# A two-layer DiT on one core: the image tokens' FFN norms spread over the context's FFN, the context's last down products moved to that FFN's end, and one modulation moved from VectorE to ScalarE

## The chip, the core and the metric

One core of one Trainium2 chip runs the whole program. Its engines work side by side and meet by semaphores: PE (TensorE: matmuls, with its weight loads as PEld), DVE (VectorE), ACT (ScalarE), POOL (GpSimd), and SP (SyncE, which issues most of the DMAs). Each engine takes its instructions in the order in which they stand in its queue. The metric is the device time of one execution in microseconds (us); lower is better. The times are medians over runs.

## The reference

Two layers work on 512 image tokens `x` and 256 context tokens `ctx`, both 1024 wide, in float32. Cut to what matters here (the mixers before it are attention, a Fourier mix and a long convolution):

```python
def conv_ffn(h, w_up, w_c, b_c, w_down):
    u = dwconv3(h @ w_up, w_c, b_c)              # 1024 -> 2 x 2816, then a 3-tap conv along the tokens
    gate, val = jnp.split(u, 2, axis=-1)
    return (jax.nn.silu(gate) * val) @ w_down    # 2816 -> 1024

for i in range(2):
    ...
    x = x + ga1 * rmsnorm(mix_x, g_post_mix[i])
    if not last:
        ctx = ctx + cga1 * rmsnorm(mix_c, g_post_mix[i])
    fx = rmsnorm(x, g_pre_ffn[i]) * (1.0 + sc2) + sh2
    x = x + ga2 * rmsnorm(conv_ffn(fx, ...), g_post_ffn[i])
    if not last:
        fc = rmsnorm(ctx, g_pre_ffn[i]) * (1.0 + csc2) + csh2
        ctx = ctx + cga2 * rmsnorm(conv_ffn(fc, ...), g_post_ffn[i])
```

In layer 0 both streams pass the FFN; the context that comes out of it is normed and modulated again at the start of layer 1 (`rmsnorm(ctx, g_pre_mix) * (1 + csc1) + csh1`). In layer 1 only x does.

## The kernel before

**Matmuls.** Each float32 operand is split into a high and a low part (L179 casts the high part on ACT, L180 subtracts it on DVE or POOL), and each product is three matmuls: high by high, high by low, low by high (`mm3`, L194 to L196). Weights come from DRAM in tiles of 512 KB (names `r`, `Wr`, `L` while raw) and become `Wh` and `Wl`. Products gather in PSUM, in four tiles `pn` and two wide tiles `pw`.

**Order of the work.** The program is written as generators. `go(name, gen, bg)` runs one of them and gives the share `bg` of PE's time to background steps ("fillers") that were put into lanes with `add`; `need(name)` runs a filler to its end before what follows. Out of the sequence so written, the framework's scheduler fixes each engine's queue when the program is built, by its own simulation. After that nothing is reordered.

**The context's FFN** (`ffn_c`, layer 0 only) takes the 22 channel blocks m of 128 in 11 groups of two. `up(m)` makes gate and value (48 matmuls with 256 columns), the convolution (L655 on ACT, L656 and L657 on DVE), SiLU, the product with the value (L1301 on POOL) and the split into `gc`. Behind the first `up` of each group come the down products of the group before (24 matmuls with 512 columns), added into `y` (L1249 on DVE). The last group's down products are not run there: `ffn_c` only makes their generator and keeps it as `rest_c`.

**What rest_c does** (`ffn_down` with `end` true): it loads two down weights (their low halves split on POOL), runs 24 matmuls, adds to `y` (L1243, DVE), takes sums of squares (L231, ACT), multiplies by the gate `G` (L1245, POOL), and then hands each of the context's two token tiles to `tail`, which adds a filler `tail_c0` or `tail_c1`. Such a filler makes the root of the mean square (L221 to L227; the square root L222 on ACT needs its own function table, loaded by ACT_TABLE_LOAD), the residual (L1155, DVE), the same for the norm that follows, a diagonal `dg` of the norm's factors (L348, DVE), and `norm_tile`: PE turns the tile by matmuls with `dg` (`turn`, L361), the modulation (scale and shift for each channel) runs on DVE (L404) or ACT (L406), and the result is split into `h`. `norm_tile(..., dve)` gives the first `dve` of each four blocks to DVE.

**The norms of x** (`norm_tile7`, fillers `norm_xf0` to `norm_xf3`, one for each 128 tokens) turn by L361, modulate on DVE (L435), and form the sums and differences that the seven-product scheme below needs (L446, L447, L449, L451, with splits by `put`, some on POOL). They are added in the mixers' output stage. What has not been run as a filler by the end of `ffn_c` is run by `need("norm_xf3")` ahead of the FFN of x.

**The FFN of x** (`ffn_x`) uses a seven-product scheme (Strassen and Winograd's): for each m, `prep(m)` makes from the up weights four differences on POOL (L1348 to L1351, `tt`), whose high and low halves are made on ACT and DVE; `first(m)` runs two of the products, `rest(m)` the other five, with sums on ACT and DVE (L1391 to L1398, tile `C`). In layer 0 the first steps are `prep(0)`, `first(0)`, `prep(1)`, `first(1)`, then `rest(0)` and `rest(1)`. `RC` in the table `Z` says where `rest_c` runs: with 3, behind `rest(3)`.

The places that the prediction speaks of are thus: `ffn_c`, the seam between it and `ffn_x`, the place of `rest_c`, and the two fillers `tail_c0` and `tail_c1`, which take their turns among the products of `ffn_x`.

Of the kernel before, what the change touches and what calls it, by code (L numbers as in the profile page):

```python
# [46 lines left out]
def tok(ap):  # L47
    return ap.rearrange("p (a t) -> p a t", t=256)
# [6 lines left out]


RT = True
Z = {'HV': [[[0], [1]], [[0, 1], []], [[], [0], [], [1]]], 'go_mod00': 1.0, 'go_norm_c': 0.3, 'go_hyp_c': 0.5, 'go_kvf_c': 0.5, 'go_q_c': 0.5, 'go_out_c': 1.0, 'go_ffn_c': 0.1, 'go_ffn': [0.1, 0.1], 'SH0': [0.7, 0.7, 0.7, 0.4, 0.5], 'SH1': [0.7, 0.7, 0.7, 0.5, 0.5], 'w_norm_x': 0.0, 'w_attn_c': 0.0, 'w_four_c': 2.0, 'w_norm_cf': 12.0, 'w_gate00': 0.0, 'w_mod_f0': 0.0, 'w_mod10': 8.0, 'w_gate10': 0.0, 'w_mod_f1': 0.0, 'w_taps': 0.0, 'mlat1': 1.0, 'mlat0': 1.2, 'mlat2': 2.0, 'lat': 7.0, 'nt': 0.8, 'nt7': 0.8, 'mg': 2.0, 'hy0': 1.0, 'hy1': 7.0, 'hy2': 14.0, 'tp0': 9.0, 'tp1': 2.5, 'tp2': 1.5, 'tp3': 2.0, 'at0': 1.5, 'at1': 2.0, 'as': 3.5, 'lead': 1, 'wx1': 9.0, 'QK0': [3.0, 7.0, 3.0, 6.0], 'QK1': [5.0, 7.0, 3.0, 6.0], 'TC': [50.0, 10.0, 10.0], 'BG': [0.15, 0.3], 'WN': [9.0, 7.0], 'ND': [3, 4], 'GF': ['Wm', 2.0, 0.0], 'MD': [4, 4, 4, 4], 'DG': [15, 15, 0], 'RC': 3, 'TW': 0.5, 'KE': 4, 'MT': 3, 'PO': [['k', 'f', 'v'], ['f', 'k', 'v']], 'EF': 1, 'E0': 4, 'lane_k': 4, 'el_na': 2, 'el_nx1': 4, 'ec': 3, 'CT': ['T', 'Q', 'T'], 'FX': 1, 'OC': 'qhHkayf'}
NF = 2, 4
OR = "", "hcyqkf"  # L60
NC = None, 4
CE = True
CR = "LL"

# [1 line left out]
class Net:  # L66
# [218 lines left out]
    def mod_block(self, l, b, out, ahead=None, tag="Wm"):  # L285
# [11 lines left out]
        out.append(s)  # L297
        yield 0.44, Z["mg"]

# [81 lines left out]
    def norm_tile(self, st, t, n, AB, el=None, dve=4):  # L381
# [14 lines left out]
        for b in range(2):  # L396
# [10 lines left out]
            for i in range(4 // kp):  # L407
                j = 4 * b // kp + i
                self.hi = self.split(hi[j][:, a, :, ts], lo[j][:, a, :, ts], tf[:, i * kp * P : (i + 1) * kp * P].rearrange("p (k t) -> p k t", t=P), el).ins
            yield 4 * CTR, Z["nt"]  # L410

    def norm_tile7(self, st, t, n, AB):
# [6 lines left out]
        def put(name, src, el):  # L419
            if name not in st.S:  # L420
                st.S[name] = tuple(self.M("h").rearrange("p (k t) -> p k t", t=256) for _ in range(2))
            hi, lo = st.S[name]
            ts = slice(t % 2 * P, t % 2 * P + P)
            self.hi = self.split(hi[:, :, ts], lo[:, :, ts], src.rearrange("p (k t) -> p k t", t=P), el).ins
# [3 lines left out]
        for b in range(2):  # L428
            ps = self.pn()
            self.turn(ps, n, b)  # L430
            for k in range(4):
                c = slice(k * P, (k + 1) * P)
                a_, b_ = A[:, 4 * b + k, st.idx : st.idx + 1], B[:, 4 * b + k, st.idx : st.idx + 1]
                if k < Z["MD"][t]:
                    self.mod = nc.vector.tensor_scalar(dst[b][:, c], ps[:, c], a_, b_, op0=ALU.mult, op1=ALU.add).ins  # L435
                else:
                    nc.scalar.activation(dst[b][:, c], ps[:, c], AF.Identity, scale=a_, bias=b_)
            if t < 2:
                put(("11", "12")[b], dst[b], (nc.gpsimd, nc.vector)[t])
            yield 4 * CTR, Z["nt7"]  # L440
        if t < 2:
# [26 lines left out]
    def norm_all(self, st, xt, AB, pre=False):  # L468
# [8 lines left out]
        for t in range(st.NT):  # L477
            yield from self.norm_tile(st, t, xt[t], AB, self.nc.vector if pre else None, Z["el_na"])

# [89 lines left out]
    def post_q(self, st, qraw, qss):  # L569
# [3 lines left out]
        st.Q = [self.M("Q").rearrange("p (h t) -> p h t", t=st.T) for _ in range(NH // hp)]  # L573
        yield 0.0, Z["QK%d" % self.lay][0] + st.NT
        pend = []
# [888 lines left out]
    def run(self):  # L1464
# [27 lines left out]
        for l in range(2):  # L1492
# [107 lines left out]
            def tail_c(t, xr, ss):  # L1600
# [176 lines left out]
```

## Time and profile before

| what | us |
|---|---|
| time, median of 3 runs | 1768.56 (1767.65 to 1769.28) |
| profiled execution | 1770.96 |
| its span | 1769.2 |
| PE busy in it | 1640.4 |
| stretch 478 to 686.8 | the context's FFN |
| stretch 686.8 to about 1065 | the FFN of x, layer 0 |

The mean granted clock of the span was 0.969. The profile names instructions by line, engine and operation, then tiles (output, arrow, inputs) and shape. In a timeline the first number is the start and the second the length; a bracket holds the idle time before it and what ended it. In a group of instructions, behind the bar stand the busy time, the mean of one in ns, then the engine's idle time just before them and its releasers. In the waits of an engine, the numbers are the total, the count and the longest.

### The profile page before, as it was taken

What the parts mean: (1) busy time and instruction counts of PE and PEld (TensorE: products, weight loads), DVE (VectorE), ACT (ScalarE), POOL (GpSimd) and SP (SyncE); (2) the same over time, 40 slices, a digit from 0 to 9 for tenths busy, and PEclk for the clock granted to TensorE, in tenths of its full rate; (3) what the DMA queues carried; (4) which work ended last, traced back from release to release, by engine and by line L of the source; (5) the groups of instructions that cost most, each with busy time, mean ns of one, the idle gap of its engine ahead of it and who ended that gap; (6) DMA issues with size and microseconds to landing.
All of it is one profiled execution on the core that took longest, in us unless ns stands there. A gap on an engine that the chain in (4) does not pass through costs nothing. (4 is left out here: it accounts for less than half of the span.)

```text
span 1769.2 us, 27894 instructions
## 1 busy us (share of the span) xinstructions
PE 1640.4 (93%) x10534; PEld 1400.9 (79%) x10534; DVE 1391.0 (79%) x2269; ACT 949.8 (54%) x1787; POOL 672.2 (38%) x495
## 2 busy tenths in 40 slices
PE   6899988899999998998899998998899799999997
PEld 2677765787788897887889985787787678999995
DVE  3776667697666698888899997668895978989996
ACT  3554354586565454555555555534874455555553
POOL 2342212000134348664465545312002456555543
PEclk9899998999999998999999998999999799999999
DMA  9224377603476642233243358654012343323323
GB/s 361 92 77 140 88 226 267 231 11 143 164 254 229 227 153 82 86 108 96 72 138 113 96 168 320 214 176 132 1 48 82 128 137 119 105 88 106 96 74 129
DMA packets 75314, 246.69 MB, mean 139 GB/s; under 512 B 8111, under 2 KB 9647, under 8 KB 75180
## 3 DMA queue, kind: packets, MB, share of 16 engines
q1 hardware_dynamic: 66348, 215.54, 36.4%
q0 software_dynamic: 8832, 29.37, 5.4%
q8 instruction: 83, 1.36, 0.3%
q14 instruction: 51, 0.42, 0.1%
HBM read 230.72 MB, written 14.16 MB: 138 GB/s over the span
## 5 line engine op out<-in xcount | busy, mean ns | idle before, releaser
L194 PE MATMUL pn<-h,Wh 128*128 128x256 f32 x1328 | 374.4, 284 | 10.9 <-DVE C L1398 3.4
L196 PE MATMUL pn<-h,Wl 128*128 128x256 f32 x1328 | 370.2, 282 | 7.6 <-DVE Wl L180 7.6
L195 PE MATMUL pn<-h,Wh 128*128 128x256 f32 x1328 | 371.9, 281 | 1.9 <-POOL h L180 1.9
L194 PEld LDWEIGHTS pn<-h,Wh 128*128 128x128 f32 x1328 | 251.8, 190 | 21.2 <-issue 4.4
L196 PEld LDWEIGHTS pn<-h,Wl 128*128 128x128 f32 x1328 | 251.3, 190 | 11.7 <-DVE Wl L180 9.0
L195 PEld LDWEIGHTS pn<-h,Wh 128*128 128x128 f32 x1328 | 252.7, 190 | 5.9 <-POOL h L180 2.1
L179 ACT CAST Wh<-Wr 128x1024 fp32r<-128x1024 f32 x118 | 123.5, 1050 | 137.3 <-PE pn L195 63.1
L1348 POOL TENSOR_TENSOR tt<-r,r 128x512 f32<-128x512 f32 x44 | 66.0, 1501 | 260.7 <-DMA r<-w_up 224.8
L180 DVE TENSOR_TENSOR Wl<-Wr,Wh 128x1024 fp32r<-128x1024 f32 x89 | 121.5, 1367 | 53.2 <-ACT Wh L179 52.7
L195 PE MATMUL pw<-Wl,gT 128*128 128x512 f32 x352 | 141.0, 401 | 2.0 <-DVE Wl L180 2.0
L194 PE MATMUL pw<-Wh,gT 128*128 128x512 f32 x352 | 136.3, 403 | 5.3 <-ACT Wh L179 2.6
L196 PE MATMUL pw<-Wh,gT 128*128 128x512 f32 x352 | 139.7, 398 | 0.0
L180 DVE TENSOR_TENSOR Wl<-tt,Wh 128x1024 fp32r<-128x1024 f32 x88 | 129.8, 1495 | 7.5 <-ACT Wh L179 7.5
L1407 POOL TENSOR_TENSOR ft<-ft,ft 128x512 f32<-128x512 f32 x44 | 66.6, 1513 | 145.0 <-DVE ft L657 78.6
L179 ACT CAST Wh<-tt 128x1024 fp32r<-128x1024 f32 x88 | 91.1, 1047 | 51.5 <-PE pw L196 32.3
L180 POOL TENSOR_TENSOR h<-tf,h 128x256 fp32r<-128x256 f32 (+1 forms) x40 | 40.3, 1028 | 177.0 <-ACT h L179 177.0
L180 POOL TENSOR_TENSOR Wl<-Wr,Wh 128x1024 fp32r<-128x1024 f32 x29 | 72.8, 2516 | 61.3 <-ACT Wh L179 61.1
L1350 POOL TENSOR_TENSOR tt<-r,tt 128x512 f32<-128x512 f32 x44 | 83.9, 1907 | 13.5 <-DVE Wl L180 13.5
L655 ACT ACTIVATE ft<-C,vec 128x512 f32<-128x512 f32 x88 | 68.9, 811 | 34.3 <-DVE C L1395 20.0
L194 PE MATMUL pw<-h,Wh 128*128 128x256 f32 (+1 forms) x224 | 76.0, 339 | 9.8 <-DVE y L1249 2.7
L292 PE MATMUL pn<-wm,cpad 128*32 128x256 f32 x768 | 69.9, 433 | 15.2 <-DMA wm<-w_mod 14.9
L1278 DVE TENSOR_TENSOR y<-y,pw 128x1024 f32<-128x1024 f32 x64 | 77.3, 1212 | 7.8 <-PE pw L196 7.7
(379 smaller groups left out, 4696.6 us busy)
## 6 DMA issues: line engine op xcount, KB each, us to landing
wm<-w_mod SPq DMA_DIRECT2D x96, 512.0 KB, 5.0
r<-w_up SPq DMA_DIRECT2D x90, 512.0 KB, 3.6
Wr<-w_down SPq DMA_DIRECT2D x66, 512.0 KB, 3.9
L<-w_up SPq DMA_DIRECT2D x44, 512.0 KB, 4.3
Wr<-w_out SPq DMA_DIRECT2D x24, 512.0 KB, 3.6
Wr<-w_in_t SPq DMA_DIRECT2D x16, 512.0 KB, 3.9
dft<-hdft_x POOLq DMA_DIRECT2D x16, 512.0 KB, 4.1
Wr<-w_in_c SPq DMA_DIRECT2D x12, 512.0 KB, 3.6
```

The lines of the kernel that those rows point to most:

```text
L179: r = nc.scalar.copy(hi, src)
L180: (el or nc.vector).tensor_tensor(lo, src, f32(hi), op=ALU.subtract)
L194: nc.tensor.matmul(ps, l[0], r[0], start=first, stop=False, **kw)
L195: nc.tensor.matmul(ps, l[0], r[1], start=False, stop=False, **kw)
L196: nc.tensor.matmul(ps, l[1], r[0], start=False, stop=last, **kw)
L292: nc.tensor.matmul(ps[32 * g : 32 * g + 32, cs], self.cpad[:, q % 2 * 4 + g, :], w[:, g, :], start=q % 2 == 0, stop=q % 2 == 1, skip_group ...
L655: nc.scalar.activation(dst, ps, AF.Identity, scale=w1, bias=b)
L1278: nc.vector.tensor_tensor(y, y, ps, op=ALU.add)
L1348: te.tensor_tensor(half(t13, 0), half(r[1], 0), half(r[0], 0), op=ALU.subtract)
L1350: te.tensor_tensor(half(t24, 0), half(r[1], 1), half(t13, 0), op=ALU.subtract)
L1407: nc.gpsimd.tensor_tensor(o[0], o[0], o[1], op=ALU.mult)
```

## The change

Three things change, all in layer 0. First, `ffn_c` calls `need("norm_xf0")` ahead of its group 1, `norm_xf1` ahead of group 3, `norm_xf2` ahead of group 5 and `norm_xf3` ahead of group 7. Second, `rest_c` is a step of its own between `ffn_c` and `ffn_x`. Third, `norm_tile` in `tail_c` gets `dve` = 0, so all four blocks of each half are modulated by ACT (L406); that is 16 instructions which move from DVE to ACT. No other instruction is added or dropped but ACT_TABLE_LOADs, of which the program has 19 now and 21 before.

```diff
-Z = {'HV': ..., 'RC': 3, ...}
+Z = {'XS': [1, 3, 5, 7], 'HV': ..., 'RC': -2, ...}
...
-NC = None, 4
+NC = None, 0
...
         groups = [list(range(a, a + G)) for a in range(0, MF, G)]
         for i, ms in enumerate(groups):
+            if i in Z["XS"]:
+                self.need(f"norm_xf{Z['XS'].index(i)}")
             for j, m in enumerate(ms):
                 yield from up(m)
...
                 self.go("ffn_c", self.ffn_c(l), Z["go_ffn_c"])
+                if Z["RC"] == -2:
+                    self.go("rest_c", self.rest_c, Z["go_ffn_c"])
                 self.need("norm_xf3")
             self.go("ffn", self.ffn_x(l), Z["go_ffn"][l])
```

In the changed kernel the lines behind the first insertion have numbers higher by 2 (L1348 becomes L1350), those behind the second by 4.

How the change moves instructions shows at three places. The first is PE's queue where x's token tile 2 is turned (`dg1032`, `y918`). Before, its first half stands here, near the end of the context's FFN, between two up products of one of its last channel blocks (`pn1334`, `pn1340`):

```order
L195 MATMUL pn1334_6606<-h968_4442,Wh1332_6602 128x256
L196 MATMUL pn1334_6606<-h966_4440,Wl1333_6603 128x256
L361 MATMUL pn1335_6634<-dg1032_4701,y918_4230 128x128 x4
L194 MATMUL pn1340_6654<-h965_4439,Wh1338_6650 128x256
L195 MATMUL pn1340_6654<-h967_4441,Wh1338_6650 128x256
```

And now the turn of tile 2, which stands some 490 rows earlier in PE's queue than it did (rows 2413 and 2418 for rows 2903 and 2928), between products of the modulation (L292) and of a middle group of the FFN:

```order
L196 MATMUL pn1217_5821<-h966_4440,Wl1216_5818 128x256
L361 MATMUL pn1218_5853<-dg1032_4701,y918_4230 128x128 x4
L292 MATMUL pn1219_5862<-wm1220_5863,cpad_79 32x256 x4
L292 MATMUL pn1219_5862<-wm1222_5878,cpad_79 32x256 x4
L194 MATMUL pw1250_5995<-Wh1245_5985,gc1200_5735 128x512
L292 MATMUL pn1219_5862<-wm1251_6002,cpad_79 32x256
L361 MATMUL pn1221_5869<-dg1032_4701,y918_4230 128x128 x4
```

The turns of all four tiles now stand in the context's FFN at rows 1917, 2164 to 2167, 2413 to 2418 and 2662 to 2663; before, all but the first half of tile 0 stood between rows 2778 and 3002, within the last 400 rows of it.

The second place is POOL's queue at the seam. `r1407`/`r1408` and `r1415`/`r1416` are the up weights of m = 0 and 1 before; `Wl1418` is the split of the latter's first half. Before:

```order
L1348 TENSOR_TENSOR tt1411_7098<-r1408_7091,r1407_7090 128x512
L1349 TENSOR_TENSOR tt1411_7098<-r1408_7091 128x512
L1301 TENSOR_TENSOR ft1378_6901<-ft1378_6901 128x256
L1350 TENSOR_TENSOR tt1412_7099<-r1408_7091,tt1411_7098 128x512
L1348 TENSOR_TENSOR tt1419_7140<-r1416_7133,r1415_7132 128x512
L1349 TENSOR_TENSOR tt1419_7140<-r1416_7133 128x512
L180 TENSOR_TENSOR Wl1418_7137<-r1415_7132,Wh1417_7136 128x1024
L1351 TENSOR_TENSOR tt1412_7099<-tt1412_7099,r1407_7090 128x512
```

Now, with `r1423`/`r1424` and `r1431`/`r1432` as the up weights of m = 0 and 1, `Wr1408` a down weight of rest_c, and `y1058`, `y1059` the context's two token tiles:

```order
L180 TENSOR_TENSOR Wl1410_7097<-Wr1408_7094,Wh1409_7096 128x1024
L1301 TENSOR_TENSOR ft1396_7015<-ft1396_7015 128x256
L180 TENSOR_TENSOR Wl1434_7197<-r1431_7192,Wh1433_7196 128x1024
L1350 TENSOR_TENSOR tt1427_7158<-r1424_7151,r1423_7150 128x512
L1351 TENSOR_TENSOR tt1427_7158<-r1424_7151 128x512
L1352 TENSOR_TENSOR tt1428_7159<-r1424_7151,tt1427_7158 128x512
L1350 TENSOR_TENSOR tt1435_7200<-r1432_7193,r1431_7192 128x512
L1351 TENSOR_TENSOR tt1435_7200<-r1432_7193 128x512
L1245 TENSOR_TENSOR y1058_4807<-y1058_4807,G1163_5510 128x512
L1353 TENSOR_TENSOR tt1428_7159<-tt1428_7159,r1423_7150 128x512
L1245 TENSOR_TENSOR y1058_4807<-y1058_4807,G1163_5510 128x512
L1245 TENSOR_TENSOR y1059_4808<-y1059_4808,G1163_5510 128x512 x2
```

Rest_c's splits now stand ahead of the differences, its four products with the gate among them, and the last product of the context's FFN with its value (L1301) ahead of all differences; before, two such products stood behind the first differences. `r1423` and `r1424` lie in the buffers of `Wr` (as `r1407` and `r1408` did before), and are loaded when rest_c's down weights have been split.

The third place is where the context's next norm is modulated. Before, it is DVE's queue in the FFN of x, between that FFN's own sums and splits (`tf` is the modulated tile):

```order
L1398 TENSOR_TENSOR C1641_8529<-pn1631_8483,C1641_8529 128x256
L404 TENSOR_SCALAR tf1667_8664<-pn1666_8659,modA936_4300,modB937_4301 128x128 x3
L180 TENSOR_TENSOR Wl1660_8639<-Wr1658_8636,Wh1659_8638 128x1024
L404 TENSOR_SCALAR tf1667_8664<-pn1666_8659,modA936_4300,modB937_4301 128x128
L404 TENSOR_SCALAR tf1670_8684<-pn1669_8679,modA936_4300,modB937_4301 128x128 x4
```

Now it is ACT's, ahead of it the square roots of both tiles behind one table load:

```order
L222 ACT_TABLE_LOAD
L222 ACTIVATE rd_y1560_7965<-ss1554_7957,rd_x1558_7963 128x1
L222 ACTIVATE rd_y1597_8169<-ss1412_7101,rd_x1595_8167 128x1
L1408 ACT_TABLE_LOAD
L1408 ACTIVATE ft1547_7925<-ft1547_7925 128x512
L179 CAST Wh1583_8130<-tt1581_8124 128x1024
L1393 COPY C1566_8019<-pn1568_8034 128x256
L179 CAST gT1549_7933<-ft1547_7925 128x512
L179 CAST Wh1592_8156<-Wr1591_8154 128x1024
L406 ACTIVATE tf1574_8082<-pn1573_8077,modB937_4301,modA936_4300 128x128 x4
L406 ACTIVATE tf1576_8107<-pn1575_8102,modB937_4301,modA936_4300 128x128 x4
```

The turns of the context's tiles on PE move with it from rows 4047 and 4277 to rows 3732 and 3890.

More of the change, by code (lines that the diff above doesn't have):

```diff
@@ L57 @@
 RT = True
-Z = {'HV': [[[0], [1]], [[0, 1], []], [[], [0], [], [1]]], 'go_mod00': 1.0, 'go_norm_c': 0.3, 'go_hyp_c': 0.5, 'go_kvf_c': 0.5, 'go_q_c': 0.5, 'go_out_c': 1.0, 'go_ffn_c': 0.1, 'go_ffn': [0.1, 0.1], 'SH0': [0.7, 0.7, 0.7, 0.4, 0.5], 'SH1': [0.7, 0.7, 0.7, 0.5, 0.5], 'w_norm_x': 0.0, 'w_attn_c': 0.0, 'w_four_c': 2.0, 'w_norm_cf': 12.0, 'w_gate00': 0.0, 'w_mod_f0': 0.0, 'w_mod10': 8.0, 'w_gate10': 0.0, 'w_mod_f1': 0.0, 'w_taps': 0.0, 'mlat1': 1.0, 'mlat0': 1.2, 'mlat2': 2.0, 'lat': 7.0, 'nt': 0.8, 'nt7': 0.8, 'mg': 2.0, 'hy0': 1.0, 'hy1': 7.0, 'hy2': 14.0, 'tp0': 9.0, 'tp1': 2.5, 'tp2': 1.5, 'tp3': 2.0, 'at0': 1.5, 'at1': 2.0, 'as': 3.5, 'lead': 1, 'wx1': 9.0, 'QK0': [3.0, 7.0, 3.0, 6.0], 'QK1': [5.0, 7.0, 3.0, 6.0], 'TC': [50.0, 10.0, 10.0], 'BG': [0.15, 0.3], 'WN': [9.0, 7.0], 'ND': [3, 4], 'GF': ['Wm', 2.0, 0.0], 'MD': [4, 4, 4, 4], 'DG': [15, 15, 0], 'RC': 3, 'TW': 0.5, 'KE': 4, 'MT': 3, 'PO': [['k', 'f', 'v'], ['f', 'k', 'v']], 'EF': 1, 'E0': 4, 'lane_k': 4, 'el_na': 2, 'el_nx1': 4, 'ec': 3, 'CT': ['T', 'Q', 'T'], 'FX': 1, 'OC': 'qhHkayf'}
+Z = {'XS': [1, 3, 5, 7], 'HV': [[[0], [1]], [[0, 1], []], [[], [0], [], [1]]], 'go_mod00': 1.0, 'go_norm_c': 0.3, 'go_hyp_c': 0.5, 'go_kvf_c': 0.5, 'go_q_c': 0.5, 'go_out_c': 1.0, 'go_ffn_c': 0.1, 'go_ffn': [0.1, 0.1], 'SH0': [0.7, 0.7, 0.7, 0.4, 0.5], 'SH1': [0.7, 0.7, 0.7, 0.5, 0.5], 'w_norm_x': 0.0, 'w_attn_c': 0.0, 'w_four_c': 2.0, 'w_norm_cf': 12.0, 'w_gate00': 0.0, 'w_mod_f0': 0.0, 'w_mod10': 8.0, 'w_gate10': 0.0, 'w_mod_f1': 0.0, 'w_taps': 0.0, 'mlat1': 1.0, 'mlat0': 1.2, 'mlat2': 2.0, 'lat': 7.0, 'nt': 0.8, 'nt7': 0.8, 'mg': 2.0, 'hy0': 1.0, 'hy1': 7.0, 'hy2': 14.0, 'tp0': 9.0, 'tp1': 2.5, 'tp2': 1.5, 'tp3': 2.0, 'at0': 1.5, 'at1': 2.0, 'as': 3.5, 'lead': 1, 'wx1': 9.0, 'QK0': [3.0, 7.0, 3.0, 6.0], 'QK1': [5.0, 7.0, 3.0, 6.0], 'TC': [50.0, 10.0, 10.0], 'BG': [0.15, 0.3], 'WN': [9.0, 7.0], 'ND': [3, 4], 'GF': ['Wm', 2.0, 0.0], 'MD': [4, 4, 4, 4], 'DG': [15, 15, 0], 'RC': -2, 'TW': 0.5, 'KE': 4, 'MT': 3, 'PO': [['k', 'f', 'v'], ['f', 'k', 'v']], 'EF': 1, 'E0': 4, 'lane_k': 4, 'el_na': 2, 'el_nx1': 4, 'ec': 3, 'CT': ['T', 'Q', 'T'], 'FX': 1, 'OC': 'qhHkayf'}
 NF = 2, 4
 OR = "", "hcyqkf"
-NC = None, 4
+NC = None, 0
 CE = True
```

## The prediction

> **What bounds the kernel now.** I read the page's busy times first, then the table of windows over the first layer's FFNs, then the waits of PE in the bad stretches, and last the timelines there.
>
> ```profile
> PE 1640.4 (93%) x10534; PEld 1400.9 (79%) x10534; DVE 1391.0 (79%) x2269; ACT 949.8 (54%) x1787; POOL 672.2 (38%) x495
> ```
>
> PE is busy 93% of the span, and matmuls are what remains if everything else is hidden. So the change is worth what it gives back of PE's idle and slow time, no more. The windows tell where that lies; the columns are length, then busy time with (x instructions) of PE, PEld, DVE, ACT and POOL, the granted clock, DMA share, GB/s.
>
> ```profile
> core 0: us, PE busy (x) PEld busy (x) DVE busy (x) ACT busy (x) POOL busy (x), PEclk, DMA share, GB/s
> 478.00:650.00 172.00, 172.00 (x1271) 151.40 (x1270) 118.89 (x192) 94.57 (x147) 70.01 (x44) 1.00 0.68 226
> 650.00:686.00 36.00, 30.21 (x211) 28.11 (x210) 35.97 (x49) 19.07 (x32) 25.33 (x14) 0.91 0.31 95
> 686.00:706.00 20.00, 17.28 (x116) 16.25 (x115) 14.50 (x17) 8.26 (x15) 13.52 (x9) 0.91 0.30 82
> 706.00:757.00 51.00, 47.15 (x334) 43.97 (x333) 43.59 (x47) 27.39 (x43) 33.60 (x19) 0.97 0.29 92
> 757.00:800.00 43.00, 38.79 (x239) 34.72 (x238) 36.66 (x40) 24.83 (x40) 27.11 (x16) 0.92 0.34 108
> 800.00:850.00 50.00, 41.16 (x256) 37.05 (x255) 41.69 (x60) 28.57 (x47) 19.60 (x14) 0.93 0.29 87
> 850.00:910.00 60.00, 56.91 (x402) 53.17 (x401) 55.37 (x77) 34.02 (x54) 33.39 (x20) 0.98 0.37 123
> 910.00:1050.00 140.00, 138.72 (x984) 129.23 (x983) 129.09 (x147) 76.17 (x122) 76.28 (x49) 1.00 0.36 114
> 650.00:910.00 260.00, 231.50 (x1549) 213.28 (x1548) 227.77 (x284) 142.14 (x229) 152.56 (x90) 0.94 0.32 101
> ```
>
> 478 to 650 is the context's FFN: PE never idle, full clock, DVE free for 53 us (172 − 118.89). From 910 x's FFN is in its rhythm and loses next to nothing. Between them, in 260 us, PE idles 28.5 us (260 − 231.50), and a clock of 0.94 costs up to 15.6 more (0.06 × 260): about 44. Row by row, idle plus slow clock: 5.8 + 3.2 = 9.0; 2.7 + 1.8 = 4.5; 3.9 + 1.5 = 5.4; 4.2 + 3.4 = 7.7; 8.8 + 3.5 = 12.3; 3.1 + 1.2 = 4.3: 43.2 in all. All three edits act in here, and what they give or take elsewhere is small.
>
> **The norms of x.** In 650:686 DVE is full (35.97 of 36), as three of x's four norms are crammed in before the FFN of x. PE then waits for a weight's low half, which DVE's queue serves too late:
>
> ```profile
> 668.12 5.15 POOL L180 TENSOR_TENSOR h<-xr,h 128x512 fp32r<-128x512 f32 x3
> 653.69 0.68 DVE L447 TENSOR_TENSOR xr<-xr 128x512 f32<-128x512 f32 x1
> 668.64 1.77 DVE L447 TENSOR_TENSOR xr<-xr 128x512 f32<-128x512 f32 x1
> 678.84 0.58 PE L196 MATMUL pn<-h,Wl 128*128 128x256 f32 x1 [4.01 <-DVE Wl L180]
> ```
>
> The change puts the four norms ahead of groups 1, 3, 5 and 7, where DVE has those 53 us free, and POOL works 70.01 of 172. The cost left there is a stall where the queue puts a tile's DVE work ahead of a Wl that PE wants. From below it is 0 (a gain is excluded: PE loses nothing there). From above, two stalls like the 4.01, which is near 7 with the second a little shorter. I take 2, nearer to zero, since DVE is 69% busy there and not 100%. Term: 9.0 becomes 2 (0 to 7).
>
> **The seam.** Between the FFNs, PE has the down products of the last groups and x's first products. rest(0), x's first full channel block, needs POOL's four differences of weights (L1348 to L1351) and their split; rest(1) four more.
>
> ```profile
> 681.02 1.73 POOL L1348 TENSOR_TENSOR tt<-r,r 128x512 f32<-128x512 f32 x1
> 686.83 0.39 PE L194 MATMUL pw<-Wh,gc 128*128 128x512 f32 x1
> 687.06 0.39 PE L195 MATMUL pw<-Wl,gc 128*128 128x512 f32 x1
> 695.32 0.39 PE L194 MATMUL pw<-h,Wh 128*128 128x256 f32 x1 [2.72 <-DVE y L1249]
> ```
>
> Before, POOL starts them at 681.02, 5.8 us before the up products of the last channel block end (686.83 begins what follows). Now rest_c comes here: 24 matmuls of 0.23 us (the step from 686.83 to 687.06) give PE 5.6 us of cover, and its POOL products stand among the differences. What POOL pays for each, from the stretch 690 to 910 (and the landing time of a down weight):
>
> ```profile
> L1350 POOL TENSOR_TENSOR tt<-r,tt 128x512 f32<-128x512 f32 x13 | 24.9, 1913 | 9.7 <-DVE Wl L180 9.7
> L1349 POOL TENSOR_TENSOR tt<-r 128x512 f32<-128x512 f32 x13 | 23.2, 1783 | 0.0
> L1351 POOL TENSOR_TENSOR tt<-tt,r 128x512 f32<-128x512 f32 x13 | 20.7, 1590 | 0.8
> L1348 POOL TENSOR_TENSOR tt<-r,r 128x512 f32<-128x512 f32 x12 | 19.4, 1619 | 49.3 <-DMA r<-w_up 41.1 <-DVE Wl L180 8.2
> L1245 POOL TENSOR_TENSOR y<-y,G 128x512 f32<-128x512 f32 x4 | 5.5, 1398 | 2.5 <-ACT junk L231 2.5
> L180 POOL TENSOR_TENSOR Wl<-Wr,Wh 128x1024 fp32r<-128x1024 f32 x2 | 5.2, 2620 | 1.1 <-ACT Wh L179 1.1
> L180 POOL TENSOR_TENSOR Wl<-r,Wh 128x1024 fp32r<-128x1024 f32 x1 | 2.8, 2815 | 0.0
> Wr<-w_down SPq DMA_DIRECT2D x4, 512.0 KB, 4.0
> ```
>
> In the new order three weight splits (2.62 + 2.62 + 2.8 = 8.0) stand ahead of the first difference, and the buffers that its weights are loaded into come free only when the two Wr splits are done; a load then lands 4.0 later. So the differences, started 5.8 before the end of up, now start between 3 before it and 4 behind it: later by 2.8 to 9.8, and I take 6. One L1245 (1.4) stands ahead of rest(0)'s last difference. The other three stand ahead of rest(1)'s last two, 4.2 more, but rest(0) covers those. The 5.6 of new PE cover is no gain in the sum, since those matmuls are only moved here. The seam's lateness is thus 6 + 1.4 = 7.4, and 4.5 becomes 12 (7 to 16: from 4.5 + 2.8, no L1245 in the way, to 4.5 + 9.8 + 1.4).
>
> Each wait here drags a slower clock behind it, and a short wait is enough:
>
> ```profile
> 728.49 0.39 PE L194 MATMUL pn<-h,w 128*128 128x256 f32 x1 [2.24 <-ACT C L1391]
> ...
> 730.00:733.40 3.40, 3.40 (x18) 3.40 (x17) 3.40 (x5) 2.14 (x3) 2.08 (x2) 0.50 0.11 45
> ```
>
> After 2.24 us of idle, PE ran 3.4 us at half clock and lost 1.7 more. The Trainium skill (TensorE: Matmul & The Clock Gate, Part 1) has the clock halved only after an idle window of about 3.4 us; by that, seam waits of 2 to 3 us each would cost no clock, and with two such stretches fewer (3.4 us) the forecast would be some 3 us lower. The trace disagrees, at 2.24, and the sum goes by the trace.
>
> **rest_c leaves x's FFN.** 706:757 has none of the change's work: 5.4 stays. 757:800 is where rest_c stood, with its four adds, its POOL products and the first residual (rows below). It loses 7.7; at its neighbour's rate (5.4 in 51) 43 us lose 4.5, which I take (3, by the pace of 850:910 with 4.3 in 60, to 7.7, nothing won).
>
> **The context's next norm.** Its residual and turn, and its modulation, now by ScalarE:
>
> ```profile
> PE pn L361 <- DVE dg L348: 5.6, 2, 4.4
> ...
> 846.67 3.78 PE L361 MATMUL pn<-dg,y 128*128 128x128 f32 x16 [4.35 <-DVE dg L348]
> ...
> 846.00:852.80 6.80, 6.13 (x28) 6.13 (x29) 5.94 (x9) 0.37 (x2) 1.85 (x1) 0.50 0.25 77
> ...
> L404 DVE TENSOR_SCALAR tf<-pn,modA,modB 128x128 f32<-128x128 f32 x16 | 5.4, 397 | 0.0
> L1155 DVE SCALAR_TENSOR_TENSOR y<-y,rd_y,xr 128x512 f32<-128x512 f32 x4 | 4.8, 1232 | 0.1
> L1243 DVE TENSOR_TENSOR y<-y,pw 128x512 f32<-128x512 f32 x4 | 2.6, 680 | 0.0
> ...
> L406 ACT ACTIVATE tf<-pn,modB,modA 128x128 f32<-128x128 f32 x32 | 13.0, 471 | 8.6 <-DVE tf L404 6.4 <-DVE rs_t L213 2.3
> L222 ACT ACT_TABLE_LOAD x10 | 12.8, 1283 | 0.3
> ```
>
> 800:910 loses 16.6 (12.3 + 4.3). The two waits for dg make 5.6 of it, and the half clock from 846 to 852.8 makes 3.4 more. In the new order the sums of squares are ready from the seam on, and both tiles' roots share one table load. I take both waits as gone: 16.6 − 9.0 = 7.6. From below, half of that (3.8), since DVE is rid of 16 × 0.34 = 5.4 us (L404) where it is 41.69 of 50 busy, and each Wl comes earlier. From above, 16.6: the turns still stand in order behind other work, and ScalarE takes VectorE's place as the one waited for. ScalarE gets 16 × 0.41 = 6.5 us (13.0 / 32) and is rid of two table loads (2.6); it is busy 62.6 of these 110 us, so I price its time at nothing. If that cover goes, each group of eight costs 3.3 on PE's path. SP's stores of the context's h go out earlier among weight loads; DMA is at 0.29 to 0.37 there, so I price them at nothing too.
>
> **The sum.** Before 9.0 + 4.5 + 5.4 + 7.7 + 16.6 = 43.2. After 2 + 12 + 5.4 + 4.5 + 7.6 = 31.5. The profiled execution took 1770.96 us; 11.7 less is 1759.3. The three timed runs have their median 2.4 lower (1768.56), so on that scale it is 1756.9: **1757**. With all the good ends (0 + 7 + 5.4 + 3 + 3.8 = 19.2) it is 1745; with all the bad ends (7 + 16 + 5.4 + 7.7 + 16.6 = 52.7) 1778.
>
> **The rivals.** *All smooth*: the low ends come together, since one cause, a VectorE with air, makes them: 1745. For it: 478:650 runs without loss at 69% DVE. Against it: 910:1050 shows full PE at 92% DVE, so DVE's load alone did not make the losses.
>
> *Tail eaten*: the turns stand behind other work in PE's queue wherever they are put, and ScalarE's modulation is served behind the casts of Wh. The tail keeps its 16.6 and rest_c's place its 7.7: 9.0 + 3.2 over the forecast, 1769, no change. For it: the dg of 846 was late though its tile was long done with its matmuls. Against: the chain is shorter by the shared load.
>
> *POOL becomes the seam's bound* (slower): the three splits wait in turn for ScalarE's Wh, and the first difference starts 8 us behind the end of up: 13.8 later than before. All four L1245 (5.6) then stand ahead of rest(1) uncovered, and two more half-clock stretches follow (3.4): 4.5 + 13.8 + 5.6 + 3.4 = 27. POOL's backlog is repeated at the next preparation (POOL is already 33.60 of 51 busy), some 5 more: 32 in place of 12, hence 1777. It decides against the change once the differences start over 5 us behind the end of up. For it: POOL's 4 + 3 + 8 operations in series are 27 us. Against: the six POOL splits of h that stood from 662 to 680 are gone from ahead of the seam (three of them took the 5.15 above).
>
> A price on that side from VectorE:
>
> ```profile
> L1155 DVE SCALAR_TENSOR_TENSOR y<-y,rd_y,xr 128x512 f32<-128x512 f32 x2 | 1.4, 750 | 0.0
> ```
>
> The residual took 750 ns in 478:650, where POOL is 41% busy, and 1232 behind 690, where it is fuller; L447 went from 0.68 to 1.77 within the POOL row above, so DVE operations on SBUF operands slow beside POOL's. The Trainium skill (SBUF — State Buffer, "SBUF: two separate sides") calls the port that the two share an exclusive lock: the later one blocks until the other is done. The trace agrees at 1.77. By it four L1245 at the seam would hold DVE's splits up by as much as 5.6 and the forecast would be 1762, within the range.
>
> **How the numbers follow.** Forecast case, 1749 to 1765: 0.52. All smooth: 0.22. Tail eaten: 0.13. POOL-bound seam: 0.13. A measurement of this kernel can tell about 0.2%, 3.5 us. Faster by more is below 1765.0: 0.52 + 0.22 = 0.74; the same 0.13; slower 0.13. The range goes from 1741 (the low end, and one 4 us stall more that goes with it) to 1771, which takes in the eaten tail and leaves out the slower case and a few hundredths below.
>
> **What would show it.** Right: in the stretch of 50 us before x's FFN, DVE well under 90% and no 4 us wait for Wl; a seam that loses about 12, with POOL's first difference near the end of up; no wait of PE for dg over 2 us; L406 x48 and no L404 in x's FFN of layer 0. Wrong: new waits of PE over 2 us within the context's FFN, or a wait for Wl or tf behind ScalarE of 3 us or more in x's FFN, or rest(0) starting over 20 us behind the last up product.

## The result and the profile after

Over 12 runs each, the changed kernel's median is 1762.07 us (1754.67 to 1768.47) and that of the kernel before 1770.41 us (1767.10 to 1778.38). The ratio is 0.9947, with a 95% interval of 0.9932 to 0.9962: 9.4 us faster, between 6.7 and 12. The profiled execution of the changed kernel took 1754.67 us, the lowest of its runs, so the two profiles differ by 16.3 us, more than the kernels do. Much of the surplus lies in the first 150 us of PE's work, before anything that the change touches: there the profile of before lost 34.4 us, and those of all thirteen other kernels of this study, the changed one among them, 28.0 to 30.0.

The windows of the changed kernel by stage. The columns are those of the prediction's table, and most stages start some 6 to 10 us earlier than their counterparts:

```profile
core 0: us, PE busy (x) PEld busy (x) DVE busy (x) ACT busy (x) POOL busy (x), PEclk, DMA share, GB/s
470.00:640.00 170.00, 167.48 (x1232) 146.46 (x1231) 129.51 (x209) 94.45 (x150) 76.48 (x48) 1.00 0.67 222
640.00:680.00 40.00, 40.00 (x284) 37.08 (x282) 26.98 (x38) 22.07 (x33) 19.15 (x10) 1.00 0.49 157
680.00:700.00 20.00, 13.30 (x73) 11.21 (x72) 15.00 (x19) 10.11 (x19) 16.70 (x12) 0.91 0.27 86
700.00:750.00 50.00, 43.97 (x317) 41.65 (x318) 44.50 (x47) 28.24 (x44) 31.53 (x17) 0.93 0.32 95
750.00:800.00 50.00, 45.76 (x320) 42.11 (x319) 43.94 (x60) 35.08 (x62) 25.80 (x17) 1.00 0.26 82
800.00:850.00 50.00, 47.71 (x332) 43.83 (x331) 44.12 (x51) 30.47 (x52) 26.92 (x18) 1.00 0.42 141
850.00:900.00 50.00, 49.18 (x348) 45.71 (x347) 46.04 (x51) 27.05 (x44) 25.75 (x17) 1.00 0.29 96
900.00:1040.00 140.00, 139.57 (x987) 128.13 (x987) 130.08 (x151) 74.84 (x117) 71.27 (x48) 1.00 0.38 123
```

The last 40 us of the context's FFN have no idle PE now and a VectorE at 67% (26.98 of 40), where it was full. The seam is worse: 6.7 us of idle in 20 and a clock of 0.91. Behind 750 the clock is at 1.00 throughout and the idle time is 4.2 + 2.3 + 0.8 = 7.3 us, where the old stretch from 757 to 910 lost 24.3 with its slow clock. The waits of PE say the same. In the context's FFN (470 to 640), around its end (640 to 700), and in the FFN of x (690 to 910), in total, times, and longest:

```profile
PE pn L196 <- DVE Wl L180: 1.7, 1, 1.7
...
PE pn L194 <- ACT Wh L179: 4.4, 4, 2.1
PE pw L194 <- DVE y L1243: 1.2, 1, 1.2
...
PE pn L361 <- DVE dg L348: 2.8, 2, 2.3
```

The norms cost one wait of 1.7 us in their new place, the 4 us wait for Wl is gone, the seam has new waits for Wh, and the turns wait 2.8 us for dg in place of 5.6. At the seam itself, GpSimd's and PE's timelines (start, length, what runs, idle time before):

```profile
678.49 0.63 PE L194 MATMUL pw<-Wh,gc 128*128 128x512 f32 x2
682.15 0.39 PE L194 MATMUL pn<-h,Wh 128*128 128x256 f32 x1 [2.10 <-ACT Wh L179]
697.44 0.39 PE L194 MATMUL pn<-h,Wh 128*128 128x256 f32 x1 [1.63 <-ACT Wh L179]
700.84 0.58 PE L196 MATMUL pn<-h,Wl 128*128 128x256 f32 x1 [1.95 <-DVE Wl L180]
...
685.54 1.47 POOL L1350 TENSOR_TENSOR tt<-r,r 128x512 f32<-128x512 f32 x1
692.87 1.29 POOL L1245 TENSOR_TENSOR y<-y,G 128x512 f32<-128x512 f32 x1
695.37 3.73 POOL L1245 TENSOR_TENSOR y<-y,G 128x512 f32<-128x512 f32 x3
...
681.05 1.99 ACT L179 CAST Wh<-r 128x1024 fp32r<-128x1024 f32 x2 [1.80 <-DMA r<-w_up]
```

The last up product ends where the row at 678.49 starts. The first difference of weights starts 7.0 us behind that (685.54); before, it started 5.8 us ahead. Even first(0) now waits 2.1 us, since its up weight lands late (ScalarE, which casts it at 681.05, had waited 1.80 us for the DMA), and rest(0) starts at 697.44 with two waits.

To compare kernels whose stages lie at other times, I lined PE's instructions up with the program and took, for each, the step to the next start, less the median step of its kind in the profile of before. The sum over a stretch is the time that PE lost there, to idling and to the slow clock. The stretches are counted in us of PE's undisturbed work. *End* is 500 to 600, the last part of the context's FFN; *seam* is 600 to 650; *next* is 650 to 700; *tail* is 700 to 800, with rest_c's old place and the context's next norm; *later* is 800 to 1025, the rest of the FFN of x and the change of layers.

| kernel | ratio to before (95%) | end | seam | next | tail | later | sum |
|---|---|---|---|---|---|---|---|
| before | | 7.4 | 11.8 | 8.6 | 17.8 | 9.6 | 55.2 |
| changed | 0.9947 (0.9932 to 0.9962) | 4.1 | 16.4 | 7.3 | 3.8 | 12.5 | 44.1 |
| norms only | 0.9979 (0.9960 to 0.9997) | 4.1 | 9.6 | 10.3 | 15.9 | 13.7 | 53.5 |
| move of rest_c only | 0.9987 (0.9970 to 1.0004) | 7.4 | 18.6 | 9.8 | 2.5 | 18.9 | 57.2 |
| ScalarE only | 0.9999 (0.9979 to 1.0019) | 7.4 | 11.2 | 8.7 | 15.2 | 9.7 | 52.2 |
| without the move | 0.9960 (0.9943 to 0.9976) | 3.6 | 8.4 | 10.9 | 15.8 | 12.4 | 51.1 |
| without ScalarE | 0.9936 (0.9913 to 0.9959) | 3.6 | 17.1 | 8.1 | 3.0 | 14.2 | 46.1 |
| without the norms | 0.9958 (0.9938 to 0.9977) | 7.4 | 17.7 | 11.1 | 2.4 | 12.3 | 50.9 |
| gate on VectorE | 0.9944 (0.9925 to 0.9962) | 4.1 | 17.2 | 8.0 | 2.0 | 13.1 | 44.3 |
| rest_c behind rest(0) | 0.9942 (0.9918 to 0.9965) | 4.1 | 18.3 | 4.4 | 7.2 | 7.8 | 41.9 |
| before, roots on VectorE | 1.0014 (0.9994 to 1.0034) | 7.3 | 11.3 | 10.3 | 16.3 | 13.6 | 58.9 |
| changed, roots on VectorE | 1.0026 (1.0006 to 1.0045) | 3.7 | 17.4 | 12.1 | 13.1 | 12.4 | 58.6 |
| third buffer | 1.0085 (1.0055 to 1.0114) | 5.0 | 17.8 | 9.6 | 14.0 | 17.6 | 64.0 |
| behind rest(0), roots on VectorE | 0.9917 (0.9889 to 0.9946) | 3.5 | 18.3 | 3.8 | 6.5 | 14.0 | 46.1 |

The last stretch ends in the midst of the change of layers, so the column *later* is the least certain. Over these five stretches the change gains 11.1 us (55.2 − 44.1); the runs say 9.4. For the others the two agree to some 6 us, which is what one profile is good for when single runs of a kernel spread over 6 to 18 us.

### The profile page after: what moved, and what is told of

Its sections match the earlier page's. It is cut to its first block, busy times and chain, and to the rows that moved or that the text cites. A ratio compares the mean times of both kernels' runs of the same rounds, so it can differ in the third digit from the quotient of the medians.

```text
span 1752.9 us, 27902 instructions
## 1 busy us (share of the span) xinstructions
PE 1626.2 (93%) x10534; PEld 1390.5 (79%) x10534; DVE 1386.7 (79%) x2253; ACT 953.2 (54%) x1801; POOL 665.6 (38%) x495
## 5 line engine op out<-in xcount | busy, mean ns | idle before, releaser
L1350 POOL TENSOR_TENSOR tt<-r,r 128x512 f32<-128x512 f32 x44 | 63.9, 1453 | 255.2 <-DMA r<-w_up 225.2
L292 PE MATMUL pn<-wm,cpad 128*32 128x256 f32 x768 | 67.9, 419 | 16.1 <-DMA wm<-w_mod 15.4
```

Source lines behind the costliest of these rows:

```text
L292: nc.tensor.matmul(ps[32 * g : 32 * g + 32, cs], self.cpad[:, q % 2 * 4 + g, :], w[:, g, :], start=q % 2 == 0, stop=q % 2 == 1, skip_group ...
L1350: te.tensor_tensor(half(t13, 0), half(r[1], 0), half(r[0], 0), op=ALU.subtract)
```

## The experiments

My theory was that the parts act each in its own place: the norms at the end of the context's FFN, the move of rest_c for the worse at the seam and for the better in the tail, ScalarE a little in the tail. Rival A: ScalarE's modulation gives the tail's time. Rival B: norms taken away from ahead of the seam make everything behind it smooth. Rival C: GpSimd is the bound at the seam. Each kernel is built anew, so each has an order of its own.

### One part at a time

Norms only is the changed kernel with these lines of before:

```diff
-Z = {'XS': [1, 3, 5, 7], ..., 'RC': -2, ...}
+Z = {'XS': [1, 3, 5, 7], ..., 'RC': 3, ...}
-NC = None, 0
+NC = None, 4
```

> Only the norms of x are spread over the context's FFN; the last down products stay behind rest(3) and VectorE modulates. Theory (each part acts in its own place): the 9 us lost in the 36 us before x's FFN fall to about 2.5, the seam stays at 4.5 and the tail at 24, so 6 to 7 us faster than before (about 1764). Rival A (ScalarE's modulation is what gives the time): also about 6 us faster, with a tail as before. Rival B (VectorE and GpSimd freed before the seam let x's weights be prepared ahead, and everything behind runs smoother): 12 us faster or more, with the tail's loss under 15.

Measured: 0.9979 (0.9960 to 0.9997), 3.7 us where 6 to 7 were expected. The end falls from 7.4 to 4.1 and the seam from 11.8 to 9.6, together 5.5 us, but 5.8 us are lost again in *next* and *later* (8.6 + 9.6 to 10.3 + 13.7). The tail keeps 15.9, with the waits for dg of before:

```profile
PE pn L361 <- DVE dg L348: 5.5, 2, 4.3
```

Rival B falls: the time is not 12 us better, and the tail's loss is not under 15.

The move of rest_c only (`'XS': []`, `'RC': -2`, `NC = None, 4`):

> Only the last down products of the context's FFN are moved to its end. Theory: the seam loses some 8 us more than before (13 in place of 4.5), the stretch behind it (from 50 us behind the seam on) some 12 less, so 3 to 5 us faster. Rival A (ScalarE's modulation gives the tail's time): the tail keeps most of its loss, so 5 us slower. Rival B: the seam's extra loss is larger than 8, since VectorE is still full of norms ahead of it, and the kernel is 0 to 5 us slower.

Measured: 0.9987 (0.9970 to 1.0004), told apart neither from no change nor from the 3 to 5 us that were expected. The seam rises by 6.8 (11.8 to 18.6) and the tail falls by 15.3 (17.8 to 2.5), though VectorE modulates; so Rival A falls here. *Later*, which holds the change of layers, takes 9 us back in this profile (9.6 to 18.9), which I had not expected.

ScalarE only (`'XS': []`, `'RC': 3`, `NC = None, 0`):

> Only the context's next norm is modulated by ScalarE. Theory: VectorE is rid of 5.4 us in the tail, the waits for dg stay: 0 to 3 us faster. Rival A: the tail's loss falls by 8 us or more, so 8 us faster. Rival B: no difference.

Measured: 0.9999 (0.9979 to 1.0019). The tail goes from 17.8 to 15.2, the 0 to 3 us of the theory's range, and the runs show nothing of it. Rival A's 8 us do not come.

### One part left out

Without the move (`'RC': 3` in the changed kernel):

> The change without the move of the last down products (they stay behind rest(3)). Theory: norms 6 to 7 and ScalarE 0 to 3 give 6 to 10 us against before, so within 3 us of the changed kernel, with the seam's loss near 5 and a tail near 20. Rival A: norms and ScalarE give all and the move costs 8 at the seam: 14 us faster than before and some 5 faster than the changed kernel. Rival B: as the changed kernel or faster, with a tail under 15.

Measured: 0.9960 (0.9943 to 0.9976), 7.1 us faster than before, as the theory has it; Rival A's 14 us do not come. The interval overlaps that of the changed kernel. In the profile the seam is 8.0 us better than with the move (8.4 against 16.4) and the tail 12.0 worse (15.8 against 3.8): the move of rest_c trades one loss for another, and its net gain is too small for these runs.

Without ScalarE (`NC = None, 4` in the changed kernel):

> The change without its third part: VectorE modulates the context's next norm. Theory (each part acts in its own place): the norms and the moved products together give 5 to 8 us against before, and ScalarE's part the rest of the changed kernel's 9, so 1 to 4 us slower than the changed kernel. Rival A (ScalarE's modulation gives the tail's time once the products are moved): 0 to 3 us faster than before at most, with the loss from 50 us behind the seam on near 20.

Measured: 0.9936 (0.9913 to 0.9959), no slower than the changed kernel, with a tail of 3.0. The 1 to 4 us of the theory do not show: the third part of the change gives nothing that these runs can tell, and Rival A is out.

Without the norms (`'XS': []` in the changed kernel):

> The change without the spread of x's norms. Theory: the 9 us ahead of x's FFN come back, 5 to 7 us slower than the changed kernel and 2 to 4 us faster than before. Rival B (the norms' removal from ahead of the seam is what makes the stretches behind it smooth): no faster than before, with the loss at the seam over 20 us.

Measured: 0.9958 (0.9938 to 0.9977). The lost time at the end is back to 7.4, with the wait of before:

```profile
671.75 0.58 PE L196 MATMUL pn<-h,Wl 128*128 128x256 f32 x1 [4.01 <-DVE Wl L180]
```

In the profile the norms are worth 6.8 us here (50.9 − 44.1), in the runs 1 permille with overlapping intervals, so the 5 to 7 us that were expected did not come. Rival B (no faster than before) falls too: the kernel is 7.4 us faster than before.

### What the seam costs

The gate products of rest_c on VectorE:

```diff
-nc.gpsimd.tensor_tensor(v, v, st.G[1][:, hs], op=ALU.mult)
+(nc.gpsimd if st is self.X else nc.vector).tensor_tensor(v, v, st.G[1][:, hs], op=ALU.mult)
```

> The change with the gate products of the context's last down products on VectorE, so that GpSimd has none of them among the differences of weights. Theory (the late start of the differences, 5.5 us behind the end of up, is what the seam costs; of the gate products only the one that stands ahead of the last difference costs): rest(0) starts 1 to 2 us earlier, 0 to 2 us faster than the changed kernel. Rival C (GpSimd is the bound of the seam, all 5.1 us of gate products count): 4 to 5 us faster.

Measured: 0.9944 (0.9925 to 0.9962), as the changed kernel. The seam loses 17.2 (16.4 with them on GpSimd), and rest(0) starts 15.8 us behind first(0), where it was 15.3 (697.44 − 682.15):

```profile
683.03 0.39 PE L194 MATMUL pn<-h,Wh 128*128 128x256 f32 x1 [2.17 <-ACT Wh L179]
698.86 0.39 PE L194 MATMUL pn<-h,Wh 128*128 128x256 f32 x1 [1.97 <-ACT Wh L179]
```

Rival C falls, and with it the slice of the theory that gave one gate product a price. GpSimd's and ScalarE's timelines show what rest(0) waits for, first in the changed kernel, then here:

```profile
694.12 1.29 POOL L1353 TENSOR_TENSOR tt<-tt,r 128x512 f32<-128x512 f32 x1
695.82 0.62 ACT L1372 COPY C<-pw 128x256 f32<-128x256 f32 x2
696.33 2.00 ACT L179 CAST Wh<-tt 128x1024 fp32r<-128x1024 f32 x2
...
694.19 1.31 POOL L1353 TENSOR_TENSOR tt<-tt,r 128x512 f32<-128x512 f32 x1
697.23 0.62 ACT L1372 COPY C<-pw 128x256 f32<-128x256 f32 x2
697.75 2.00 ACT L179 CAST Wh<-tt 128x1024 fp32r<-128x1024 f32 x2
```

GpSimd is done with the last difference of m = 0 at 695.4 and 695.5. The cast of its high part comes 0.9 and 2.2 us later, when ScalarE's queue reaches it: ahead of it stand rest_c's sums of squares, a table load with a root, and the copies of x's first products, without idle time from 692.4 on in the changed kernel and from 693.8 on here. So it is ScalarE's queue, not GpSimd's, that lets rest(0) start last; no run moved the cast to try it.

The last down products behind rest(0) (`'RC': 0` in the changed kernel), so that their weights do not hold the buffers that x's first weights need:

> The change with the context's last down products behind rest(0) in place of ahead of x's FFN; norms spread and ScalarE as in the change. Theory (at the seam the buffers that the last down weights hold make the differences late): the buffers of the first weights come free earlier, the differences start before the end of up, rest(0) starts some 12 us behind that end in place of 17, and the seam's loss falls from 13 to about 6: 3 to 7 us faster than the changed kernel. Rival C (the products are needed as cover at the seam): the same or slower.

Measured: 0.9942 (0.9918 to 0.9965), as the changed kernel. The first half of it came as expected: the differences start early, in GpSimd's timeline,

```profile
672.69 1.33 POOL L1350 TENSOR_TENSOR tt<-r,r 128x512 f32<-128x512 f32 x1 [3.30 <-issue]
```

and the first 25 us of the seam's stretch lose 2.0 in place of 13.0. But the second 25, where rest_c stands now, lose 16.3 in place of 3.4, with waits like these two for a low part that VectorE makes:

```profile
707.49 0.58 PE L196 MATMUL pn<-h,Wl 128*128 128x256 f32 x1 [2.28 <-DVE Wl L180]
721.60 0.58 PE L196 MATMUL pn<-h,Wl 128*128 128x256 f32 x1 [2.87 <-DVE Wl L180]
```

The cost goes with rest_c, so the 3 to 7 us of the theory do not come. In its tail the ScalarE modulation shows up as a wait, which it does in no other kernel here:

```profile
805.95 0.58 PE L194 MATMUL pn<-h,Wh 128*128 128x256 f32 x1 [5.48 <-ACT tf L406]
```

A third buffer for the raw down weights and the first up weights, at the cost of the small tiles:

```diff
-BUFS = {"M": 27, "T": 5, ..., "Wr": 2, ...}
+BUFS = {"M": 27, "T": 3, ..., "Wr": 3, ...}
```

> The changed kernel with three buffers in place of two for the raw down weights and the first up weights (and three in place of five for the small work tiles, to make room). One of the two first up weights can then be loaded before the last down weights are split; the other still waits. Theory (the differences start 5.5 us behind the end of up because of these buffers): they start 1 to 4 us earlier, and the loss at the seam falls from 13 to about 10; the smaller work pool may cost as much elsewhere: 3 us faster to 2 slower. Rival C (GpSimd's queue is the bound): the seam as in the changed kernel.

Measured: 1.0085 (1.0055 to 1.0114), slower than before and some 24 us slower than the changed kernel, where 3 us faster to 2 slower was expected. The seam's first half lost 8.5 in place of 13.0, as the theory has it, and its second half 9.3 in place of 3.4. The smaller pool is mixed into that and into the rest, so the run says little on the buffers. It says something on the tail, though: it loses 14.0, with the longest wait for dg but one in this study:

```profile
828.07 2.07 PE L361 MATMUL pn<-dg,y 128*128 128x128 f32 x8 [9.17 <-DVE dg L348]
```

### What the wait for dg is

In the profile of before, ScalarE loads the root's table twice ahead of the late dg (at 837.77 and 841.32, with the SiLU's table at 839.38 between them), and VectorE waits for the second root:

```profile
841.32 1.28 ACT L222 ACT_TABLE_LOAD   x1
...
842.94 0.16 DVE L225 RECIPROCAL rd_y<-rd_y 128x1 f32<-128x1 f32 x1 [3.12 <-ACT rd_y L222]
```

In the changed kernel the two roots share one load. That seemed to be the tail's gain, so I took the loads away: `tail_c` makes its four roots by VectorE's iteration (L204 to L214), which takes nine small VectorE operations a root in place of six.

```diff
-        r = self.rstd(ss)
+        r = self.rsqrt(ss[:, 0:1], D, ss[:, 1:2]) if vec else self.rstd(ss)
...
-                n = self.norm_diag(Cx.y[t], xr)
+                n = self.norm_diag(Cx.y[t], xr, True)
```

In the kernel before:

> The kernel before, with one thing changed: the four roots of the context's tail (two residuals, two norms) are made by VectorE's own iteration in place of ScalarE's square root, so no function table is loaded for them (8 table loads fewer, each 1.28 us; VectorE gets 4 small operations more for each root). Theory (the wait of 4.35 us for dg comes from the two table loads in a row ahead of the two roots, with VectorE waiting 3.1 us behind them; moving the products brings both roots under one load): the wait for dg falls from 4.35 to under 2 us and the loss of 17.8 us in this stretch by 5 to 9, so 5 to 8 us faster than before. Rival D (the stretch loses its time because rest_c's adds, residual and turns collide with the products of m = 3 to 8 wherever the roots are made): the wait moves on and the time is within 2 us of before.

Measured: 1.0014 (0.9994 to 1.0034). Of the 4.35 us, 3.96 stay, and the tail loses 16.3 as before (17.8):

```profile
848.36 3.26 PE L361 MATMUL pn<-dg,y 128*128 128x128 f32 x16 [3.96 <-DVE dg L348]
```

VectorE has no idle time for a root any more, but PE waits nearly as long, so my theory that the loads make the wait falls. What the loads cost by themselves is not shown, as the iteration adds links to the chain. In the changed kernel:

> The changed kernel with the same roots on VectorE (6 table loads fewer). Theory: the wait of 2.3 us for dg that is left falls to about 1, and the chain of the first residual at the seam no longer waits 1.3 us for ScalarE: 1 to 3 us faster than the changed kernel. Rival D: the same.

Measured: 1.0026 (1.0006 to 1.0045), 14 us slower than the changed kernel. The first tile's turn no longer waits, but the second's waits 10.3 us, and the tail loses 13.1 in place of 3.8. VectorE's timeline ahead of it, and GpSimd's beside it:

```profile
819.04 1.24 DVE L214 SCALAR_TENSOR_TENSOR rs_y<-rs_t,rs_y 128x1 f32<-128x1 f32 x1
825.41 0.15 DVE L214 SCALAR_TENSOR_TENSOR rs_y<-rs_t,rs_y 128x1 f32<-128x1 f32 x1
828.70 1.21 DVE L214 SCALAR_TENSOR_TENSOR rs_y<-rs_t,rs_y 128x1 f32<-128x1 f32 x1
829.95 1.25 DVE L348 TENSOR_SCALAR dg<-ident,rs_y 128x128 f32<-128x128 f32 x1
```

```profile
818.53 1.73 POOL L1351 TENSOR_TENSOR tt<-r 128x512 f32<-128x512 f32 x1
827.59 2.31 POOL L1350 TENSOR_TENSOR tt<-r,r 128x512 f32<-128x512 f32 x1
829.86 1.26 POOL L1351 TENSOR_TENSOR tt<-r 128x512 f32<-128x512 f32 x1
```

```profile
831.25 2.07 PE L361 MATMUL pn<-dg,y 128*128 128x128 f32 x8 [10.26 <-DVE dg L348]
```

The chain has more links now. Other work of VectorE stands between the links, and PE has come to the turn ten microseconds before dg is there. So this wait follows from where the builder put the turn in PE's queue against the chain in VectorE's, with no load of ScalarE in it. GpSimd adds to it: three of the four rows of VectorE above, and a step of the chain at 822.48 (1.22 us), ran beside one of its operations. Against 0.15, 0.21 and 0.28 us for such steps alone (825.41 here, 816.07 here, the dg of 846.34 in the profile of before), that is some 4 of the 10.3 us, an estimate from these rows.

Last, the products behind rest(0), VectorE modulating, roots on VectorE:

> Norms spread over the context's FFN, the last down products behind rest(0), VectorE modulating, roots on VectorE. Theory: the seam's loss is small (2 in place of 13), the stretch from 25 to 200 us behind it loses some 5 less than with the products there and the square roots: 12 to 16 us faster than before, 3 to 6 faster than the changed kernel. Rival D: as the kernel with the products behind rest(0), 10 us faster than before.

Measured: 0.9917 (0.9889 to 0.9946), 14.7 us faster than before and the fastest here by its middle; its interval overlaps that of the changed kernel. Its tail loses 6.5, with one wait for dg of 2.1 us, though the same roots cost 10.3 in the kernel above. The theory's time came out, but the two runs before do not bear out its reason (cheaper roots); what is left is the order of the queues, which was not tried by itself.

## Why the prediction was right, and where its steps were off

**Direction and size.** Forecast 1757 with 1741 to 1771, measured 1762.07; forecast 11.7 us gained within the profile, measured 9.4 by the ratio. The forecast case was the one that came. The closeness is in part luck. By the windows the terms were 2.5 + 18.0 + 7.3 = 27.8 where 31.5 was forecast, and a loss at the change of layers that had no term stands against that. The 2.4 us taken off for the median of three runs are not borne out either: over 12 runs the median of before is 1770.41, next to its profiled execution.

**The norms of x.** 9.0 was to become 2 (0 to 7). The two windows up to 680 lose 2.5 now, with one stall of 1.7. Right. Alone the norms are worth 3.7 us in the runs, so about half of the term was lost again further on, where the prediction had nothing written down for it.

**The seam.** 4.5 was to become 12, and 706:757 to keep 5.4: 17.4. Measured, 680 to 750: 6.7 + 1.8 + 6.0 + 3.5 = 18.0. The sum is right but its derivation is not, so that it came out is in part luck. The shift of the differences was put at 6 us (2.8 to 9.8); it was 12.8 (from 5.8 ahead of the last up product's end to 7.0 behind). The gate product that was given 1.4 us gave nothing back when it was moved to VectorE. The step that failed is the path: I let rest(0) wait for GpSimd's last difference, and the rows show it waiting for ScalarE's queue, where rest_c's sums and root stand ahead of the cast. PE's first products and rest_c's matmuls covered more of the lateness than I had allowed. That is also why the slower rival failed although its condition came true: the differences did start over 5 us behind the end of up, and its price, all four gate products and two more slow stretches, did not follow.

**rest_c's place and the tail.** 4.5 + 7.6 = 12.1 was forecast behind the seam; the windows from 750 to 900 lose 7.3. The two waits for dg were to go; 2.8 of 5.6 us stayed, and the longest is 2.3, above the 2 that I had named as the sign. But the other waits went with them, and the granted clock is 1.00 all through, so the term came out better than forecast. The reason that I gave, ready sums of squares and one shared table load, is not enough: the kernel with the third buffer has both, three loads for four roots as in the changed kernel, and waits 9.2 us, and taking the loads away did not take the wait away. Two kernels with rest_c at the seam (third buffer, roots on VectorE) have a tail of 13 to 14 like those without the move, so the move alone does not give a smooth tail. What the rows show in the late chains is other work of VectorE between the links. That the order of the queues decides is argued from this, and why the builder's order is better in the other five was not tried apart; the term's gain is in part luck of that order.

**ScalarE.** I counted 5.4 us off VectorE as a reason for the low end only, and ScalarE's time at nothing. With and without it the ratios are 0.9947 and 0.9936, and alone 0.9999: nothing that these runs can tell. The moved work itself is as the change says, 48 modulations in ScalarE's line where there were 32:

```profile
L406 ACT ACTIVATE tf<-pn,modB,modA 128x128 f32<-128x128 f32 x48 | 18.9, 468 | 9.2 <-PE pn L361 5.8 <-DVE rs_t L213 2.3 <-DVE tf L404 1.2
```

**What was missing** is the change of layers: *later* went from 9.6 to 12.5. PE comes there 20 us earlier in the profile, and waits 3.2 us for the next modulation's weights where it had waited 1.4. More comes from the tiles that ScalarE scales (L378) for the next turns. The rows are the changed kernel's, then, last, the wait of before:

```profile
1059.83 0.64 PE L292 MATMUL pn<-wm,cpad 128*32 128x256 f32 x8 [3.16 <-DMA wm<-w_mod]
PE pn L359 <- ACT y L378: 5.4, 2, 3.2
...
PE pn L359 <- ACT y L378: 0.6, 1, 0.6
```

Other waits there became shorter; all of PE's waits in these 70 us went from 8.9 to 11.7 us. Why the scaled tiles come late was not tried.

## What to carry to other kernels

Move work from a stretch where its engine is full to one where PE never idles and the engine has air, and look for waits further on: here about half of that term came back as such. A tail of work that is moved takes its cost along: look at both places, at which buffers its weights hold there, and at what then stands ahead of the next casts in each queue. For a short chain that PE waits for, count the links and what stands between them in each queue before blaming the one long step in it; the way to know is to take that step away.

## What the runs showed of the hardware

A VectorE operation on 128x1 elements took 0.15 us alone and 1.24 and 1.21 us beside GpSimd, and it ended each time with GpSimd's operation: 819.04 + 1.24 = 820.28 against 818.53 + 1.73 = 820.26, and 828.70 + 1.21 = 829.91 against 827.59 + 2.31 = 829.90. The Trainium skill (SBUF — State Buffer, "SBUF: two separate sides") has the port that the two share as an exclusive lock, held for a whole instruction; these rows agree, to 0.02 us. The other profiles bear it out: of 312 such operations, with 128x1 elements and two inputs, that began while one of GpSimd's ran, 265 ended within 0.05 us of its end. So the smallest operation can pay the most, in proportion, and a chain of small ones beside a busy GpSimd is slow.

The clock did not fall after each wait of 2 us. In the profile of before it was at 0.50 for 3.4 us after an idle time of 2.24 us; in the changed kernel it stayed at 1.00 after one of 2.32 us (the turn at 782.50):

```profile
782.50 2.05 PE L361 MATMUL pn<-dg,y 128*128 128x128 f32 x16 [2.32 <-DVE dg L348]
...
782.50:789.50 7.00, 7.00 (x58) 6.90 (x59) 7.00 (x9) 5.14 (x13) 3.53 (x3) 1.00 0.01 2
```

The length of the gap alone does not decide. The Trainium skill (TensorE: Matmul & The Clock Gate, Part 1) says that the activity window runs free of the kernel, so that the point of the switch depends on where in the window the first matmul falls. The traces agree on the free-running window: in all fourteen profiles every change of the granted clock lies on a grid of 3.41 us. Cut on that grid, the two gaps differ (before, the window ahead of the half clock and the next one; then two windows of the changed kernel, around the gap at 782.50):

```profile
726.58:729.99 3.41, 1.50 (x12) 1.50 (x13) 3.41 (x6) 3.41 (x7) 0.00 (x0) 1.00 0.80 261
729.99:733.40 3.41, 3.41 (x18) 3.41 (x17) 3.41 (x5) 2.15 (x3) 2.08 (x2) 0.50 0.12 47
...
778.26:781.67 3.41, 1.92 (x15) 1.67 (x13) 3.41 (x6) 1.95 (x4) 3.41 (x4) 1.00 0.00 0
781.67:785.09 3.42, 2.59 (x22) 2.59 (x23) 3.42 (x5) 2.46 (x7) 1.97 (x2) 1.00 0.02 5
```

The gap of 2.24 us put 1.91 us of idle time into one window; that of 2.32 us was shared out as 1.49 and 0.83. From 300 us on, the fourteen profiles hold 166 windows at full clock that were followed by one at half clock, and PE had been idle for 1.4 to 3.4 us in each of them; in the 5440 that were followed by another at full clock, it had been idle for at most 1.9. So it is the idle time within one window that goes with the half clock, and about half a window was enough.
